# Two blocks and a routed expert layer on one core: one fixed first expert instead of two, the order of the others worked out earlier, twelve weight slots, a new order of passes

## The chip, the core and the metric

One core of a Trainium2 chip runs one program. The metric is its time in microseconds on the device. Engines: TensorE (PE; its weight loads are listed as PEld), VectorE (DVE), ScalarE (ACT), GpSimd (POOL) and the sync engine (SP), which issues the large loads. Transfers run on 16 DMA engines.

## What is computed

`reference` runs two blocks over 512 rows of 1024. The first mixes a gated convolution and a linear recurrence, the second is attention followed by an expert layer. The change is in the expert layer, which is in essence:

```python
logits = h @ w_router + b_router                     # 512 rows, 32 experts
top_val, top_idx = top_k(logits, 4); gates = softmax(top_val)
# the rows of each expert, 2048 places in all
hgu = xs @ w_gate_up[e] + b_gate_up[e]               # 1024 x 2048
act = clamped_swiglu(hgu)
out = (act @ w_down[e] + b_down[e]) * gate           # 1024 x 1024
h = layernorm(alpha * h + sum over the 4 experts of out)
```

Inputs and outputs are float32. Each expert has 12 MB of weights, so the layer reads 32 x 12 MB.

## The kernel before

**Passes.** The expert stage runs 32 passes, one for each expert. Passes 0 and 1 are experts 0 and 1 (STATIC = 2). The other 30 experts are put in order of their number of rows, and each place in that order (rank) is given to a pass of a fixed kind by a table (`moe`, from `_tables`, line 42): the two ranks with most rows go to PAIRS (8, 18), the next ten to large passes, then 15 to SMALL and the last three to TINY. Kinds differ in rows and in arithmetic. A large pass holds 128 rows; each weight tile is split by ScalarE (line 128) and VectorE (line 129) into a high and a low part, and three products are summed (`products`, lines 1894 to 1920). A small pass holds 64 rows and a tiny one 32; they multiply the raw float32 tile and put the column blocks side by side in the array (`small_products`, line 1867). A pair is a large pass with a further tiny tile of 32 rows on the same raw weights. An expert with more rows than its pass holds gets further tiles in a loop at the end (`further_tiles`, line 1979).

**Units and their order.** A pass has a way up (gate and up weights, 8 units of 1 MB) and a way down (4 units of 1 MB). Block b of the loop at line 2048 runs the way up of pass b and then the way down of pass b - 1 (`units`, line 282). So the weights are used in the order: up 0, up 1, down 0, up 2, down 1 and so on. `beside` (line 1924) puts the other steps of neighbouring passes before or in the middle of a unit's products: `place` and `fetch` (which rows), `gather` (an indirect load on the POOL queue), `xpose` and `xparts` (transposing the rows on TensorE and copying them), `glu`, `at_T` and `at_parts` (the gate function and the transposed activations), `finish` (scaling by the gate on ScalarE, then a scatter-add to memory on the POOL queue). Each engine works through its own instructions in the order written.

**Weights.** `Weights` (line 86) holds a list of loads to do and a list of free raw slots of 1 MB. `issue` takes the first load and the first slot and issues the load on the sync queue; it is called when a slot is released. A large pass releases a raw slot when the tile is split, a small or tiny one after the unit's products, a pair after the products of both tiles. `ahead` and `beyond` split up to two units ahead into three pairs of split buffers. There are RAW + RAWK + RAWX = 2 + 7 + 2 = 11 slots; the last two lie in the pool `pM`, whose memory is free once the attention's residual has been stored.

**The order of the experts.** `order` (line 1643) runs in steps beside pass 0: it compares all 32 x 32 keys (count x 32 - index) in one VectorE operation, sums them to ranks, turns ranks and counts into columns by TensorE, builds a permutation matrix and permutes the lists. Its result `pm_i` is read by the sync engine (`expert`, line 1969) for the address of each load of an ordered pass, first for unit 20. Rows of passes 0 and 1 are gathered ahead of the loop (lines 1562, 2036 to 2040), so the rows of pass 1 are there before pass 0 begins.

## Time and profile before

| | us |
|---|---|
| median of 3 runs (1916.35 to 1921.56) | 1917.02 |
| the profiled execution | 1921.13 |
| its span, first to last instruction | 1919.4 |
| busy: TensorE, VectorE, ScalarE, POOL | 1723.4, 1153.2, 774.8, 512.7 |
| read from and written to memory | 488.8 MB and 20.1 MB |

All rows are from the profiled execution, in microseconds from the start of its span. A busy TensorE includes the time that a matmul is drawn out by what it waits for inside, so a busy share near 100% doesn't say that it runs at its peak. "DMA share" is the busy share of the 16 DMA engines; overlapping packets make it exceed 1 slightly. The granted clock of TensorE has a mean of 0.951 of full speed over the span.

### The profile page before, as it was taken

How to read it: one execution, taken by the hardware profiler on the slowest of the kernel's cores; microseconds unless marked ns; L12 is line 12 of the kernel's file. 1: busy time of each engine (PE TensorE's matmuls, PEld its weight loads, DVE VectorE, ACT ScalarE, POOL GpSimd, SP SyncE). 2: the span in 40 equal slices, each digit the busy share in tenths (PEclk: the TensorE clock that was granted, in tenths of full speed). 3: DMA queues.
4: the chain of work that ended last, by engine and by line, in shares of the span. 5: the costliest groups of instructions: out<-in, count | busy, mean ns of one | idle time of the engine just before them, and what ended most of it. 6: DMA issues, size and time to landing. Idle time of an engine off the chain costs nothing. (4 is left out here: it accounts for less than half of the span.)

```text
span 1919.4 us, 23312 instructions
## 1 busy us (share of the span) xinstructions
PE 1723.4 (90%) x8751; PEld 1144.0 (60%) x8751; DVE 1153.2 (60%) x1448; ACT 774.8 (40%) x910; POOL 512.7 (27%) x400
## 2 busy tenths in 40 slices
PE   4899886979898899899998898999989899999995
PEld 3687664758787677776552455456445565767531
DVE  6799984775746556798440444347345466767513
ACT  5223533733335444364420333335233354556301
POOL 3899995540311221401101001011010110101002
PEclk8999898989998899899999898999999999999998
DMA  8322221254221005688999999999998999999994
GB/s 296 88 72 71 77 88 59 95 198 154 89 61 55 1 1 177 263 310 326 410 396 395 389 350 378 404 403 406 402 387 340 384 406 411 405 395 406 376 408 160
DMA packets 127508, 503.52 MB, mean 262 GB/s; under 512 B 15350, under 2 KB 57908, under 8 KB 79776
## 3 DMA queue, kind: packets, MB, share of 16 engines
q1 hardware_dynamic: 115568, 475.22, 63.5%
q0 software_dynamic: 11088, 25.39, 4.8%
q8 instruction: 70, 1.15, 0.2%
q10 hardware_dynamic: 736, 1.38, 0.2%
q14 instruction: 46, 0.38, 0.1%
HBM read 488.80 MB, written 20.10 MB: 265 GB/s over the span
## 5 line engine op out<-in xcount | busy, mean ns | idle before, releaser
L129 DVE TENSOR_TENSOR wlo<-wraw,whi 128x2048 fp32r<-128x2048 f32 (+1 forms) x213 | 486.5, 2292 | 161.6 <-ACT whi L128 151.7
L128 ACT CAST whi<-wraw 128x2048 fp32r<-128x2048 f32 (+1 forms) x213 | 401.7, 1891 | 172.0 <-PE pg L1907 56.4
L1889 PE MATMUL pg<-wraw,xTs 128*64 128x512 f32 (+1 forms) x1600 | 259.1, 514 | 4.9 <-DMA wraw<-w_gate_up 4.8
L1889 PEld LDWEIGHTS pg<-wraw,xTs 128*64 128x64 f32 (+1 forms) x1600 | 82.7, 126 | 150.5 <-issue 117.8
L1618 DVE TENSOR_SCALAR lp<-pg 128x512 f32<-128x512 f32 (+1 forms) x48 | 31.6, 659 | 195.7 <-ACT sg L1617 195.7
L1889 PE MATMUL pg<-wraw,ats 128*64 128x512 f32 (+1 forms) x800 | 141.0, 528 | 8.7 <-issue 5.4
L1907 PE MATMUL pg<-whi,xTh 128*128 128x512 f32 x448 | 127.7, 407 | 13.4 <-ACT whi L128 13.4
L1548 POOL DMA_INDIRECT xg<-h_d,ix x34 | 57.9, 1702 | 284.2 <-issue 109.4
L544 POOL TENSOR_TENSOR acc<-acc,sparel 128x512 f32<-128x512 f32 x91 | 129.1, 1419 | 7.7 <-ACT acc L533 0.2
L1625 POOL DMA_INDIRECT acc_d<-y,back x19 | 30.2, 1591 | 371.6 <-ACT y L1861 312.0
L1907 PE MATMUL pg<-whi,xTl 128*128 128x512 f32 x448 | 125.5, 402 | 0.0
L1907 PE MATMUL pg<-wlo,xTh 128*128 128x512 f32 x448 | 122.4, 395 | 0.0
L1907 PEld LDWEIGHTS pg<-whi,xTh 128*128 128x128 f32 x448 | 83.3, 192 | 41.5 <-ACT whi L128 14.3
L1625 POOL DMA_INDIRECT acc_d<-y,ix x14 | 25.1, 1793 | 298.2 <-ACT y L1864 235.5
L537 DVE SCALAR_TENSOR_TENSOR pc<-v,C,pc 128x512 f32<-128x512 f32 x144 | 101.6, 747 | 2.1 <-ACT pc L533 0.8
L1617 ACT ACTIVATE sg<-pg 128x512 f32<-128x512 f32 (+1 forms) x48 | 26.4, 574 | 189.2 <-PE pg L1889 114.4
L542 POOL TENSOR_SCALAR sparel<-v,C 128x512 f32<-128x512 f32 x91 | 97.9, 1076 | 14.8 <-DVE V L459 6.2
L1907 PEld LDWEIGHTS pg<-wlo,xTh 128*128 128x128 f32 x448 | 85.2, 190 | 19.3
L1907 PEld LDWEIGHTS pg<-whi,xTl 128*128 128x128 f32 x448 | 84.0, 192 | 17.8 <-issue 0.4
L1889 PEld LDWEIGHTS pg<-wraw,ats 128*64 128x64 f32 (+1 forms) x800 | 39.6, 127 | 78.5 <-issue 56.7
L1918 PE MATMUL pg<-whi,ath 128*128 128x512 f32 x224 | 75.6, 419 | 1.6 <-ACT whi L128 1.6
L1918 PE MATMUL pg<-wlo,ath 128*128 128x512 f32 x224 | 71.7, 402 | 3.1 <-DVE wlo L129 3.0
(662 smaller groups left out, 3336.8 us busy)
## 6 DMA issues: line engine op xcount, KB each, us to landing
wraw<-w_gate_up SPq DMA_DIRECT2D x256, 1024.0 KB, 17.7
wraw<-w_down SPq DMA_DIRECT2D x128, 1024.0 KB, 18.7
wraw<-w_in SPq DMA_DIRECT2D x17, 1024.0 KB, 5.3
wraw<-w_out SPq DMA_DIRECT2D x8, 1024.0 KB, 5.0
mraw<-mod_w SPq DMA_DIRECT2D x7, 1024.0 KB, 15.5
wraw<-w_in SPq DMA_DIRECT2D x14, 512.0 KB, 5.3
wraw<-pw_w SPq DMA_DIRECT2D x4, 1024.0 KB, 5.1
wraw<-mod_w SPq DMA_DIRECT2D x4, 1024.0 KB, 5.0
```

The costliest lines, as they stand in the source:

```text
L128: self.nc.scalar.copy(out=hi[:, c], in_=t[:, c])
L129: self.nc.vector.tensor_tensor(out=lo[:, c], in0=t[:, c], in1=hi[:, c].bitcast(F32), op=OP.subtract)
L537: dve.scalar_tensor_tensor(out=acc[:, c, :] if j == 29 and not np_ else st_["o"], in0=v[:, j:j + S], scalar=dw_col(j, c), in1=st_["o"], op ...
L542: pool.tensor_scalar(out=pr_, in0=v[:, j:j + S], scalar1=dw_col(j, c), scalar2=0.0, op0=OP.mult, op1=OP.add)
L544: pool.tensor_tensor(out=acc[:, c, :], in0=acc[:, c, :], in1=pr_, op=OP.add)
L1548: pool.indirect_dma_start(out=xg, out_offset=None, in_=h1_d[:, :], in_offset=bass.IndirectOffsetOnAxis(ap=ix[0:w], axis=0), bounds_check=S ...
L1617: act.activation(out=sg, in_=v2[:, :, :, 0], func=AF.Sigmoid, scale=1.702)
L1618: dve.tensor_scalar(out=lp, in0=v2[:, :, :, 1], scalar1=-6.0, scalar2=8.0, op0=OP.max, op1=OP.min)
L1625: pool.indirect_dma_start(out=dst, out_offset=bass.IndirectOffsetOnAxis(ap=ix, axis=0), in_=y, in_offset=None, bounds_check=nt * S - 1, oo ...
L1889: pe.matmul(o, l, t[:, c0:c0 + n_], start=False, stop=u == 3 and k == 1 if dn else u == 7)
L1907: pe.matmul(it["acc"][c // 2][:, c % 2, :], l, r[:, 512 * c:512 * c + 512], start=False, stop=u == 7 and j == 2)
L1918: pe.matmul(it["acc"][2][:, c, :], l, r[:, c0:c0 + 512], start=False, stop=end)
```

## The change

1. STATIC is 1: only expert 0 has a fixed pass. The other 31 experts are ordered; the new table has pairs at passes 3 and 9, tiny passes at 1, 4 and 10, 16 further small ones, and large ones at 5, 7 and then at every odd pass from 11 to 25. There are ten ordered large passes as before, and one more small one.
2. The ranks are worked out ahead of the gates, by one comparison of a row of keys with a column of keys (the counts also come as a column, from 16 one-column matmuls), and `pm_i` is there before the loop. `order` keeps only the permutation of the lists.
3. The way down of pass 0 is loaded right behind its way up, ahead of the way up of pass 1 (`late` gives a load's place in the order of use); the loads of all later passes are listed before the loop.
4. RAWX is 3, so there are 12 raw slots; row buffers, one product buffer and the row parts have one copy less, and a pair's second tile has an output buffer of its own (`yt`).
5. The rows of pass 1 are gathered in block 0 (gather ahead of unit 5, transposes in the middle of unit 7, copies behind it), no longer ahead of the loop. The gates of pass 0 follow ahead of unit 5.

The diff without its context lines:

```diff
@@ -32,10 +32,10 @@
-STATIC = 2
-PAIRS = (8, 18)
-SMALL = (2, 3, 5, 6, 7, 9, 11, 12, 14, 16, 17, 19, 21, 23, 26, 29, 30, 31)
-TINY = (2, 9, 19)
+STATIC = 1
+PAIRS = (3, 9)
+SMALL = (1, 2, 4, 6, 8, 10, 12, 14, 16, 18, 20, 22, 24, 26, 27, 28, 29, 30, 31)
+TINY = (1, 4, 10)
@@ -73,13 +73,17 @@
-    moe = np.zeros((128, 66), f)
+    moe = np.zeros((128, 67 + NE), f)
+    least = np.arange(NE) + 131072.0 * (np.arange(NE) < STATIC)
+    moe[:, 66] = least[p % NE]
+    moe[:, 67:] = least
@@ -91,26 +95,34 @@
-    def add(self, *loads, split=True, n=2048, pieces=1):
-        self.todo.append((loads, split, n, pieces))
+        self.last, self.used = 0, 0
+    def add(self, *loads, split=True, n=2048, pieces=1, late=0):
+        self.todo.append((loads, split, n, pieces, self.last + late))
+        self.last += 1
+    def ready(self):
+        return self.raw and self.raw[0][-1] == self.used
     def issue(self):
-        loads, split, n, pieces = self.todo.pop(0)
+        loads, split, n, pieces, at = self.todo.pop(0)
-        self.raw.append((t, split, n, pieces, slot))
+        self.raw.append((t, split, n, pieces, slot, at))
+        self.raw.sort(key=lambda r: r[-1])
     def split(self):
-        t, s, n, pieces, slot = self.raw.pop(0)
+        t, s, n, pieces, slot, _ = self.raw.pop(0)
+        self.used += 1
@@ -138,12 +150,12 @@
     def ahead(self, n):
-        while len(self.part) < n and self.raw:
+        while len(self.part) < n and self.ready():
     def beyond(self, n):
-        while self.raw and len(self.part) < n:
+        while self.ready() and len(self.part) < n:
@@ -206,7 +218,7 @@
-    RAW, RAWK, RAWX = 2, 7, 2
+    RAW, RAWK, RAWX = 2, 7, 3
@@ -296,18 +308,23 @@
     def rows2(w, pairs):
-    def add_unit(p, dn, u, of):
+    def add_unit(p, dn, u, of, late=0):
         def src():
-        W.add((kn(2, 1024) if dn else flat, src), split="both" if p in PAIRS else p not in SMALL)
+        W.add((kn(2, 1024) if dn else flat, src), split="both" if p in PAIRS else p not in SMALL,
+              late=late)
-    for p in range(STATIC):
-        add_block(p, lambda e: (w_gu[e], w_dn[e]))
+    FIRST = lambda e: (w_gu[0], w_dn[0])
+    for p, dn, u in units(0):
+        add_unit(p, dn, u, FIRST)
+    for u in range(4):
+        add_unit(0, True, u, FIRST, 8)
...
@@ -1491,6 +1508,10 @@
+    for j in range(4):
+        for i in range(4):
+            pe.matmul(pp_[NE * i:NE * i + NE, 5 * NE:5 * NE + 1], sel[:, j, :], trib[:, 1, 0:1], start=(j == 0),
+                      stop=(j == 3))
@@ -1560,9 +1581,29 @@
+    pmr = pK.tile([128, NE], F32, name="pmr")
+    pm_i = pK.tile([1, NE], I32, name="pm_i")
+    Pk = pK.tile([128, NE], F32, name="Pk")
+    pcol = pK.tile([128, 2], F32, name="pcol")
+    ky = lrep.rearrange("p i e -> p (i e)")
+    key, gtr, kc = ky[:, 0:NE], ky[:, NE:2 * NE], ky[:, 2 * NE:2 * NE + 1]
+    dve.tensor_copy(out=pcol[:, 1:2], in_=pp_[:, 5 * NE:5 * NE + 1])
+    dve.scalar_tensor_tensor(out=key, in0=cnt, scalar=float(NE), in1=moe[:, 67:], op0=OP.mult, op1=OP.subtract)
+    dve.scalar_tensor_tensor(out=kc, in0=pcol[:, 1:2], scalar=float(NE), in1=moe[:, 66:67], op0=OP.mult,
+                             op1=OP.subtract)
+    dve.tensor_scalar(out=gtr, in0=key, scalar1=kc, scalar2=None, op0=OP.is_gt)
+    dve.tensor_reduce(out=pcol[:, 0:1], in_=gtr, axis=mybir.AxisListType.X, op=OP.add)
+    dve.tensor_scalar(out=Pk, in0=moe[:, 0:NE], scalar1=pcol[:, 0:1], scalar2=None, op0=OP.is_equal)
+    pp1 = psa("pperm")
+    pe.matmul(pp1[:, 0:NE], sq5[0:NE, 4, 65:66].to_broadcast([NE, 128]), Pk[0:NE], start=True, stop=True)
+    pe.matmul(pp1[:, NE:2 * NE], pcol[0:NE, 1:2].to_broadcast([NE, 128]), Pk[0:NE], start=True, stop=True)
+    dve.tensor_copy(out=pm_i, in_=pp1[0:1, 0:NE])
+    dve.tensor_copy(out=pmr, in_=pp1[:, 0:NE])
+    dve.tensor_copy(out=cnt, in_=pp1[:, NE:2 * NE])
@@ -1602,8 +1643,7 @@
-    def transposed(xg, a):
-        pt = psa("pxt")
+    def transposed(xg, a, pt):
@@ -1613,7 +1653,7 @@
-        lp = pM.tile([128, 2, 256], F32, tag="lp", name="lp", bufs=2)[:, 0:a, 0:n]
+        lp = pM.tile([128, 2, 256], F32, tag="lp", name="lp")[:, 0:a, 0:n]
@@ -1636,46 +1676,20 @@
     def into(parts, k, src):
-    pmr = pK.tile([128, NE], F32, name="pmr")
-    pm_i = pK.tile([1, NE], I32, name="pm_i")
     def order():
-        io = sq5[:, 4, 1:1 + NE]
-        key, r = [wk[:, NE * j:NE * j + NE] for j in range(2)]
-        pcol = wk[:, 7 * NE + 2:7 * NE + 4]
-        Pk, Pb, pT = wk[:, 256:288], wk[:, 288:416], wk[:, 512:768]
-        rows = wk[:, 768:1024]
-        gt_ = pM.tile([128, NE, NE], BF16, tag="xi", name="gt_")
-        pt = psa("pord")
+        Pb, pT = wk[:, 288:416], wk[:, 512:768]
+        pt = pss("pord")[:, 0, :]
-        dve.scalar_tensor_tensor(out=key, in0=cnt, scalar=float(NE), in1=io, op0=OP.mult, op1=OP.subtract)
-        for e in range(STATIC):
-            dve.memset(key[:, e:e + 1], -float(NE * (e + 1)))
-        yield
-        dve.tensor_tensor(out=gt_, in0=key.unsqueeze(1).to_broadcast([128, NE, NE]),
-                          in1=key.unsqueeze(2).to_broadcast([128, NE, NE]), op=OP.is_gt)
+        yield
-        yield
-        dve.tensor_reduce(out=r, in_=gt_, axis=mybir.AxisListType.X, op=OP.add)
-        for j, row in enumerate((r, cnt)):
-            dve.tensor_copy(out=rows[0:1, 128 * j:128 * j + 128].rearrange("p (i e) -> p i e", i=4),
-                     in_=row[0:1].unsqueeze(1).to_broadcast([1, 4, NE]))
-        yield
-        pc = psa("pcol")
-        for j in range(2):
-            pe.matmul(pc[:, j:j + 1], rows[0:1, 128 * j:128 * j + 128], ones[0:1, 0:1], start=True, stop=True)
-        dve.tensor_copy(out=pcol, in_=pc[:, 0:2])
-        dve.tensor_scalar(out=Pk, in0=moe[:, 0:NE], scalar1=pcol[:, 0:1], scalar2=None, op0=OP.is_equal)
-        pe.matmul(pp2[:, 0:NE], sq5[0:NE, 4, 65:66].to_broadcast([NE, 128]), Pk[0:NE], start=True, stop=True)
-        pe.matmul(pp2[:, NE:2 * NE], pcol[0:NE, 1:2].to_broadcast([NE, 128]), Pk[0:NE], start=True, stop=True)
@@ -1685,9 +1699,6 @@
-        dve.tensor_copy(out=pm_i, in_=pp2[0:1, 0:NE])
-        dve.tensor_copy(out=pmr, in_=pp2[:, 0:NE])
-        dve.tensor_copy(out=cnt, in_=pp2[:, NE:2 * NE])
@@ -1769,7 +1780,7 @@
     def fetch(n):
-        it["pi"] = rows_at(it["oh"], it["cols"], 0, 5 if n > 1 else 2)
+        it["pi"] = rows_at(it["oh"], it["cols"], 0, 5)
@@ -1779,8 +1790,7 @@
-        if n > 1:
-            it["gt"] = gates_of(it["pi"])
+        it["gt"] = gates_of(it["pi"])
@@ -1788,21 +1798,25 @@
     def xpose(n):
-        it["pt"] = transposed_rows(it["xg"]) if small(n) else [transposed(it["xg"], a) for a in range(2)]
-    def x_tile(n=9):
-        return xT_[n] if n < 2 else [pM.tile([128, 8, 128], F32R, tag=t, name=t, bufs=2) for t in ("xTh", "xTl")]
+        if small(n):
+            it["pt"] = transposed_rows(it["xg"])
+        else:
+            pt = pss("pxt") if n == 0 else None
+            it["pt"] = [transposed(it["xg"], a, pt[:, a, :] if n == 0 else psa("pxt")) for a in range(2)]
+    def x_tile():
+        return [pM.tile([128, 8, 128], F32R, tag=t, name=t) for t in ("xTh", "xTl")]
     def xparts(n):
-            xp = pM.tile([128, 8, 128 // small(n)], F32, tag="xTh", name="xTs", bufs=2)
+            xp = pM.tile([128, 8, 128 // small(n)], F32, tag="xTh" if small(n) == 2 else "xTs", name="xTs")
-        xp = x_tile(n)
+        xp = x_tile()
...
@@ -1855,7 +1869,7 @@
     def finish(n):
-        y = pM.tile([128, D], F32, tag="y", name="y")
+        y = pM.tile([128, 256], F32, tag="yt", name="y") if PLACES[n][1] else pM.tile([128, D], F32, tag="y", name="y")
@@ -1944,15 +1958,19 @@
-            before[7] += [(late_gates, 0), (late_gates, 1), (place, 2)]
-            midst[7].append((fetch, 2))
-            midst[4].append((xpose, 1))
-            before[5].append((xparts, 1))
+            before[4].append((place, 1))
+            midst[4].append((fetch, 1))
+            before[5] += [(gather, 1), (late_gates, 0)]
+            before[8].append((place, 2))
+            midst[7].append((xpose, 1))
+            before[8].append((xparts, 1))
-                if j or b == 1 and n != 2:
+                if j:
+                if b == 1:
+                    midst[1].append((fetch, n))
...
@@ -2030,21 +2048,21 @@
-    xT_ = [[pM.tile([128, 8, 128], F32R, tag=t, name=t, bufs=2) for t in ("xTh", "xTl")] for _ in range(2)]
-    place(1)
-    fetch(1)
-    gather(1)
+    for p, dn, u in units(1):
+        if not dn:
+            add_unit(p, dn, u, of, -4)
+    for b in range(2, NE + 1):
+        add_block(b, of)
-    next(ordering)
@@ -2087,9 +2105,6 @@
-                if j == 6:
-                    for n in range(STATIC, NE + 1):
-                        add_block(n, of)
```

## Rows read from the trace of the kernel before

**Rows 1.** The page: memory traffic in 40 slices of 48 us.
```profile
GB/s 296 88 72 71 77 88 59 95 198 154 89 61 55 1 1 177 263 310 326 410 396 395 389 350 378 404 403 406 402 387 340 384 406 411 405 395 406 376 408 160
```

**Rows 2.** Stretches: length, busy time by engine, clock, DMA share, GB/s.
```profile
815.00:850.00 35.00, 30.86 (x153) 23.35 (x151) 30.76 (x39) 19.86 (x16) 0.17 (x1) 0.99 0.85 314
850.00:894.00 44.00, 44.00 (x296) 33.20 (x298) 37.44 (x49) 25.23 (x24) 4.29 (x3) 1.00 0.79 291
894.00:1080.00 186.00, 165.61 (x814) 77.54 (x807) 74.83 (x98) 48.62 (x52) 20.50 (x15) 0.94 1.02 401
1080.00:1130.00 50.00, 48.21 (x382) 27.57 (x383) 22.10 (x27) 16.48 (x20) 5.33 (x3) 1.00 0.90 327
1130.00:1420.00 290.00, 269.67 (x1388) 147.99 (x1381) 138.72 (x149) 107.63 (x101) 32.29 (x20) 0.96 1.01 401
1420.00:1470.00 50.00, 48.21 (x389) 27.41 (x391) 22.10 (x27) 16.50 (x20) 4.94 (x4) 1.00 0.87 316
...
1640.00:1780.00 140.00, 139.78 (x650) 94.16 (x649) 103.92 (x96) 80.99 (x68) 15.39 (x8) 1.00 1.00 399
1780.00:1800.00 20.00, 20.00 (x99) 11.79 (x99) 9.83 (x14) 6.38 (x10) 1.57 (x1) 1.00 0.91 354
...
757.00:1882.00 1125.00, 1060.36 (x5703) 621.39 (x5701) 606.34 (x711) 441.41 (x419) 132.13 (x83) 0.97 0.97 380
```

**Rows 3.** DMA queue of the loads, 1640:1780: packets, MB, share.
```profile
q1 hardware_dynamic: 7366, 53.62, 93.9%
```

**Rows 4.** Stretches: large up, pair up, large down, small up, down.
```profile
1755.20:1778.60 23.40, 22.76 (x96) 17.82 (x96) 1.00 1.02 399
1079.10:1112.60 33.50, 24.34 (x96) 17.40 (x96) 1.00 0.93 343
...
1778.70:1791.30 12.60, 11.81 (x48) 8.79 (x48) 1.00 1.01 419
...
1793.00:1808.70 15.70, 14.39 (x64) 4.33 (x64) 1.00 0.90 315
1839.00:1847.10 8.10, 7.31 (x32) 2.12 (x32) 1.00 1.01 422
```

**Rows 5.** Timeline of the sync queue: start, length, line, count.
```profile
873.96 15.21 SPq L105 DMA_DIRECT2D wraw<-w_down  x4
890.03 9.80 SPq L105 DMA_DIRECT2D wraw<-w_gate_up  x8
```

**Rows 6.** DMA issues, whole run and at 868.4: median us to landing.
```profile
wraw<-w_gate_up SPq DMA_DIRECT2D x256, 1024.0 KB, 17.7
...
wraw<-w_gate_up SPq DMA_DIRECT2D x1, 1024.0 KB, 5.4
```

**Rows 7.** Gather issued at 863.94: us to landing; TensorE's timeline.
```profile
xg<-h_d,ix POOLq DMA_INDIRECT x1, 7.5
...
905.23 1.08 PE L1602 MATMUL pxt<-sq,xg 64*128 64x64 f32 x8 [4.51 <-DMA xg<-h_d,ix]
...
1071.78 1.05 PE L1602 MATMUL pxt<-sq,xg 32*128 32x32 f32 x8 [6.85 <-DVE xTl L201]
```

**Rows 8.** Timeline ahead of the first products: VectorE, TensorE.
```profile
811.09 0.29 DVE L1505 TENSOR_REDUCE gs<-rt 128x4 f32<-128x128 f32 x1
...
819.93 0.66 PE L1608 MATMUL pxt<-sq,xg 128*128 128x128 f32 x4 [1.87 <-DVE xTl L201]
...
821.18 1.20 PE L1907 MATMUL pg<-whi,xTh 128*128 128x512 f32 x4
```

**Rows 9.** POOL's DMA queue, 813:822, 899.9:904.9, 893:898: packets, MB.
```profile
q0 software_dynamic: 288, 0.38, 15.7%
...
q0 software_dynamic: 80, 0.26, 17.9%
...
q0 software_dynamic: 139, 0.13, 14.6%
```

**Rows 10.** Timeline of ScalarE behind the first pair.
```profile
1162.66 0.47 ACT L1861 ACTIVATE y<-pg,gt 128x256 f32<-128x256 f32 x1 [11.14 <-DMA acc_d<-y,ix]
```

More of the change, by code (lines that the diff above doesn't have):

```diff
@@ L1335, in block_kernel @@
     xg2 = [pK.tile([128, D], F32, name=f"xg{i}") for i in range(2)]
-    moe = pK.tile([128, 66], F32, name="moe")
+    moe = pK.tile([128, 67 + NE], F32, name="moe")
     sp.dma_start(out=moe, in_=A["t_moe"])
@@ L1836, in at_parts @@
                 if n == NI - 1:
-                    it["at"] = pM.tile([128, 8, 128], F32, tag="xTh", name="ats", bufs=2)[:, 0:4]
+                    it["at"] = pM.tile([128, 8, 128], F32, tag="xTl", name="ats")[:, 0:4]
                 elif PLACES[n][1]:
@@ L2001, in further_tiles @@
                 se = oer.to_broadcast([128, 128])
-                xT = pM.tile([128, 8, 128], F32R, tag="xTh", name="xTf", bufs=2).bitcast(F32)
+                xT = pM.tile([128, 8, 128], F32R, tag="xTh", name="xTf").bitcast(F32)
                 for a in range(2):
-                    k, src_ = transposed(xg, a)
+                    k, src_ = transposed(xg, a, psa("pxt"))
                     act.copy(out=xT[:, k, :], in_=src_)
```

## The prediction

> **What bounds the kernel now.** I read the slices of the page first: from slice 18 (816 us) to the slice before the last the GB/s line stands at 310 to 411 [rows 1]. So the expert stage, over half of the span, moves weights nearly all the time. The chain of waits that the page gives covers only the last dozen microseconds and says nothing of that stage. I cut the stage into stretches instead [rows 2]. There are two kinds. In the full ones (894:1080, 1130:1420, 1640:1780) the DMA share is 1.00 to 1.02 at 399 to 401 GB/s. In the others it falls: 815:850, 850:894, 1080:1130, 1420:1470, 1780:1800. One weight unit is 1.049 MB; 53.62 MB in the 140 us of the fullest long stretch is 51.1 units, 2.74 us each, gathers and scatters included [rows 3]. There are 384 units. The stage ends when the last has landed (about 1882), and the 37 us from there to the end of the span are untouched by the change.
>
> Second, how near TensorE is. A large pass takes 23.4 us for its way up and 12.6 for its way down, a small one 15.7 and 8.1, a pair 33.5 for its way up [rows 4]. 12 units at 2.74 take 32.9 us. So a small pass (23.8) and a large beside a small (59.8 against 65.8) wait for DMA, two larges and a small (95.8 with the gaps of about 0.5 us: 99) just exceed it (98.7), and a pair's way up (4.19 us a unit) is far slower than DMA. DMA is the bound, and what can be won is DMA time that stands empty because every raw slot holds something. Against 401 GB/s the stretches lose: 815:850 (1 - 314/401) x 35 = 7.6 us; 850:894 12.1; 1080:1130 9.2; 1420:1470 10.6; 1780:1800 2.3. Together 41.8 us. DMA also rests ahead of 815, until the last pool's slots exist; the change keeps that.
>
> **The change part by part.** *Early part of the stage.* Before, passes 0 and 1 are both large and hold a split weight each 2.9 us, so units are issued at about that pace; pass 2, a tiny one, frees its eight slots only from 887 on, and the queue, which issues four units in 15 us from 873.96, issues eight in the 10 us from 890.03 [rows 5]. After, pass 1 is tiny and runs right behind pass 0's way up: 821.18 [rows 8] + 23.4 [rows 4] + 3.4 (next paragraph) + 2 for the row parts, near 850. Units 0 to 7 (way up), 8 to 11 (way down, loaded ahead) and 12 to 19 (pass 1) fill the slots: seven are freed by pass 0's splits, one more is the twelfth. They land by about 847, as the nineteenth does now. Then nothing can be issued until pass 1 frees its first slot, near 851.5; with 5.4 us from issue to landing on an empty queue [rows 6] unit 20 lands near 857. From there I take 2.7 us a unit. So of 850:894 I keep about 5 us and win 7. The twelfth slot is worth one unit in 815:850: 2.6 us.
>
> The price of this order is a shorter way for pass 1's rows. Their gather stands ahead of unit 5 and TensorE's transposes of them in the middle of unit 7, 2.3 units (6.7 us) later. The gather's VectorE steps come behind a split, about 1.4 us into the unit, the POOL instruction 1.1 us on, and 7.5 us to landing [rows 7]: 10 us together. So TensorE waits about 3.4 us there, with two thirds of unit 7 and all of pass 1 queued behind it, and VectorE and ScalarE (the gate functions) behind those. This is in the 850 above. The second such wait, for pass 2's rows in pass 0's way down, replaces the one that is there now, 4.51 us [rows 7].
>
> *The ordering of the experts.* It adds ten small VectorE operations of at most 0.29 us each [rows 8], with a trip over TensorE (two small matmuls) that VectorE waits for, ahead of the gates, and 16 one-column matmuls. It lies under the gather of pass 0's rows. Against it, pass 1's one-hot and index no longer stand ahead of the two splits, and both transposes go into one large PSUM tile, so that the second no longer waits 1.87 us [rows 8]. No row shows the new chain: from 1.87 us sooner to 4 us later (2.9 and an estimated 1 for the trip) for the first product. I take 0, as the gather and the warming matmuls cover most of it; if that cover is gone, the 4 us fall on the early part. The sync queue now reads the order before unit 12, not 20; behind that read stand all later loads. The list should be ready near 814, the last pool's slots come at 815, so it costs nothing; without that cover it delays every load by what it is late.
>
> *One large pass becomes small.* TensorE loses 36.0 - 23.8 = 12 us of work, which alone wins nothing where DMA is the bound. The bytes stay: 32 experts are read in full. The extra-tile loop stays empty: pass 3 gathers 0.26 MB, 64 rows of 4 KB, so rank 12 exactly fills its 64 places; expert 1 has at most 60 rows (both fixed passes gather 0.38 MB, 92 rows, of which pass 0 scatters 32, 0.13 MB [rows 9]) and falls in behind it.
>
> *The pairs.* After, they stand at 3 and 9. A unit takes 17.7 us from issue to landing when the queue is full [rows 6], so about six are in flight and, of 11 slots, five hold landed units when a pair begins; its way up of 33.5 us then takes eight of the 12 units that DMA could bring. The new pass 3 starts near 897 (850, a tiny way up of some 9, 12.6 and 4.5 for pass 0's way down, 15.7, 5) with about four landed and eight of 12 slots in flight, two more than now: 9.2 - 2 x 2.74 = 3.7 stay. At pass 9 only the twelfth slot helps: 10.6 - 2.6 = 8. Won: 8.1 us. The output buffer of its own for a pair's second tile takes away a ScalarE wait of 11.14 us behind each pair [rows 10], which held up the next large pass; the DMA queue stayed full there (1130:1420 at 401), so I count nothing, and behind pass 3 it helps TensorE catch up.
>
> *The order behind them.* Large and small alternate from 11 to 25 and six small ones end it, so two larges never stand together: the 2.3 us of 1780:1800 go. The single buffers for rows and products are rewritten only after their readers in the same engine's order: nothing.
>
> **The sum.** 2.6 + 7 + 8.1 + 2.3 = 20 us. The profiled execution took 1921.1 (span 1919.4); 1901 for it. The median is 4.1 lower, so 1897.
>
> At one place a rule speaks against this. The full stretches read and write 399 to 401 GB/s for up to 290 us [rows 2]. The Trainium skill, "DMA: Bandwidth & Descriptors", Specifications, gives about 358 GB/s as the limit of HBM for one core. By it the 427 MB of 757:1882 (1125 us at 380 GB/s) would take 1193 us, more than the 1125 measured, and there would be no empty time to win; the trace disagrees, and its 401 is used; the second rival below has the same time.
>
> **The rivals.**
> *Half of it is given back* (0.16): pass 3 keeps its 9.2 us and the waits for rows take 5 more of the early part; 20 - 5.5 - 5 = 9.5 us, 1907. For it: waits of 4.51 and 6.85 us in TensorE's order behind other engines [rows 7]. Against: each is under three units.
> *The mean rate can't rise* (0.13): the whole stage holds 380 GB/s [rows 2]; if memory or the queue caps the mean near it, or units come at 2.8 us once DMA never rests, 330 units lose 20 us: 1917, no change. Against: three stretches of 140 us and more at 399 to 401.
> *Slower* (0.07): a large pass whose first split waits for its landing holds ScalarE, so the row parts, so TensorE's transposes: 6.85 us now, ahead of pass 8 [rows 7]. From 11 to 25 the new order has eight larges, each behind a small or tiny one. If at each the slots fill meanwhile, 8 x 6.85 = 55 us more: 1897 + 55 = 1952. It decides when such a wait exceeds what is in flight: seven units of 2.74, less two, 14 us. None in the trace comes near, and the stretch with the 6.85 kept 401 GB/s.
> *Everything empty goes* (0.05): 1917 - 41.8 = 1875.
>
> **How the numbers follow.** My forecast has 0.59; its own range is 1886 to 1907: 0.02 us a unit over some 330 units is 7, the ordering's ends are 2 and 4. The range given, 1881 to 1914, leaves out the slower rival, part of the flat one and the best case. About 0.3% (6 us) is what a measurement here tells from no change. Faster: 0.59 + 0.05 + 0.12 of the halved gain; same: 0.13 + 0.04; slower 0.07.
>
> **What would show it.** After: units landing at 2.7 us without a break from about 857; no stretch under 360 GB/s but one near pass 9; TensorE waiting some 3 us for gathered rows near 845; no ScalarE wait of 11 us behind a pair; the last unit landing near 1862. I am wrong if DMA still stands at 290 GB/s before 895, if a full stretch falls under 390, or if work of the extra-tile loop appears.

## The result, and the profile after

| | before | changed |
|---|---|---|
| median (four runs each, side by side) | 1918.76 us | 1892.58 us |
| ratio, 95% interval | | 0.9858 [0.9841, 0.9875] |
| the same again, other runs (nine and four) | 1919.77 us | 1894.87 us, 0.9857 [0.9839, 0.9876] |
| profiled execution, its span | 1921.13, 1919.4 us | 1887.72, 1885.8 us |

The forecast was 1897, 20 us less than before; it came out at 26.2 us less (24.0 to 30.5 by the interval). Below, a kernel's distance from the changed one is taken from 1893.4 us, the median of its eight runs. Each ratio has an interval of some 0.0015 to either side, 3 us, so a difference between two experiments holds to about 4 us.

The slices of the page, kernel after (memory traffic, 47 us each): the dips of [rows 1] at 350, 387, 340, 384 and 376 are gone. The eighteenth slice reads 265 where it read 310, but it covers 801 to 849 now and covered 816 to 864 before; the stretches below have the same bounds in both, and the stage begins 5.3 us sooner now.

```profile
GB/s 301 90 73 73 78 90 45 112 135 213 59 104 56 1 1 110 298 265 365 390 395 412 399 413 398 403 403 411 420 402 406 404 404 396 403 406 396 406 414 132
```

Stretches of the kernel after, columns as in [rows 2] (length, busy time by engine, granted clock, DMA share, GB/s):

```profile
815.00:850.00 35.00, 29.69 (x158) 21.69 (x160) 18.76 (x28) 14.06 (x14) 2.81 (x1) 0.95 0.66 259
850.00:894.00 44.00, 39.39 (x300) 19.85 (x292) 27.00 (x47) 13.27 (x15) 4.73 (x4) 1.00 0.97 376
894.00:1080.00 186.00, 182.06 (x1190) 109.08 (x1192) 110.61 (x127) 79.13 (x78) 26.47 (x16) 0.99 1.00 398
930.00:950.00 20.00, 18.35 (x151) 8.01 (x153) 7.04 (x13) 3.50 (x8) 1.63 (x1) 1.00 0.89 345
1080.00:1130.00 50.00, 48.49 (x314) 32.07 (x311) 31.64 (x23) 25.99 (x19) 4.16 (x2) 1.00 1.01 413
1130.00:1420.00 290.00, 282.22 (x1531) 165.98 (x1530) 166.75 (x171) 129.68 (x121) 34.44 (x19) 0.99 1.02 407
1420.00:1470.00 50.00, 50.00 (x239) 31.44 (x239) 30.88 (x32) 22.13 (x22) 6.25 (x3) 1.00 1.01 400
...
1780.00:1800.00 20.00, 16.47 (x72) 4.50 (x68) 0.00 (x0) 0.75 (x2) 2.57 (x2) 1.00 1.02 399
```

Against 401 GB/s, as in the prediction, what stands empty is 12.4 us in 815:850, 2.7 in 850:894, 2.8 in 930:950 (behind the pair at pass 3) and 0.1 in 1780:1800: 18.0 us where it was 41.8. So 23.8 of the 33.6 us between the two profiled spans are empty DMA time that is gone. Another 5.3 come from ahead of the stage: the first weight load is issued at 751.75 instead of 757.02, which the change doesn't cause (last section). From that issue to the last landing the stage takes 1097.5 us instead of 1125.4, 28.0 less, so some 4 are left beside the 23.8; 1130:1420, at 407 GB/s instead of 401, is worth 4.3, and the other stretches gain or lose some 1.5 us each.

What waits for what has turned over. The sums of waits of the kernel before, and of the one after (engine, line, waited for: us in total, times, longest):

```profile
ACT whi L128 <- DMA wraw<-w_down: 26.5, 10, 9.3
ACT whi L128 <- DMA wraw<-w_gate_up: 20.4, 4, 7.9
ACT y L1861 <- DMA acc_d<-y,ix: 21.7, 2, 11.1
```
```profile
ACT whi L140 <- DMA wraw<-w_down: 73.8, 27, 8.7
PEld pg L1903 <- DMA wraw<-w_gate_up: 33.1, 31, 3.0
POOL acc_d L1665 <- DMA acc_d<-y,ix: 17.5, 2, 9.1
```

The splits and the small products now stand waiting for the experts' weights to land more than before: 73.8 against 26.5 and 20.4 us for the splits. ScalarE's wait for the scatter behind the pairs is gone; it is now POOL, about to issue the next scatter, that waits for it. More of the stage is limited by DMA than before.

### The profile page after: what moved, and what is told of

The parts are those of the page before. It is cut to its first block, busy times and chain, and to the rows that moved or that the text cites. A ratio compares the mean times of both kernels' runs of the same rounds, so it can differ in the third digit from the quotient of the medians.

```text
span 1885.8 us, 23223 instructions
## 1 busy us (share of the span) xinstructions
PE 1701.9 (90%) x8713; PEld 1111.8 (59%) x8713; DVE 1118.5 (59%) x1425; ACT 751.9 (40%) x894; POOL 516.0 (27%) x400
## 5 line engine op out<-in xcount | busy, mean ns | idle before, releaser
L141 DVE TENSOR_TENSOR wlo<-wraw,whi 128x2048 fp32r<-128x2048 f32 (+1 forms) x201 | 457.0, 2282 | 152.9 <-ACT whi L140 146.7
L140 ACT CAST whi<-wraw 128x2048 fp32r<-128x2048 f32 (+1 forms) x201 | 379.6, 1891 | 193.6 <-DMA wraw<-w_down 73.8
L1903 PE MATMUL pg<-wraw,xTs 128*64 128x512 f32 (+1 forms) x1664 | 274.6, 516 | 12.0 <-DMA wraw<-w_gate_up 12.0
L1903 PE MATMUL pg<-wraw,ats 128*64 128x512 f32 (+1 forms) x832 | 145.0, 524 | 6.3 <-DMA wraw<-w_down 3.8
L1921 PE MATMUL pg<-whi,xTh 128*128 128x512 f32 x416 | 116.2, 401 | 0.4 <-issue 0.4
L1921 PE MATMUL pg<-whi,xTl 128*128 128x512 f32 x416 | 114.8, 398 | 0.0
L1921 PE MATMUL pg<-wlo,xTh 128*128 128x512 f32 x416 | 113.2, 394 | 0.0
L1657 ACT ACTIVATE sg<-pg 128x512 f32<-128x512 f32 (+1 forms) x47 | 25.7, 573 | 184.3 <-PE pg L1903 101.1
L1921 PEld LDWEIGHTS pg<-whi,xTh 128*128 128x128 f32 x416 | 75.9, 188 | 26.0 <-issue 10.6
L1921 PEld LDWEIGHTS pg<-wlo,xTh 128*128 128x128 f32 x416 | 78.7, 189 | 17.7
L1921 PEld LDWEIGHTS pg<-whi,xTl 128*128 128x128 f32 x416 | 76.6, 188 | 16.3
L213 DVE TENSOR_TENSOR atl<-pat,ath 128x256 fp32r<-128x256 f32 x52 | 20.0, 421 | 92.4 <-ACT ath L212 92.4
## 6 DMA issues: line engine op xcount, KB each, us to landing
wraw<-w_gate_up SPq DMA_DIRECT2D x256, 1024.0 KB, 20.4
```

Of the source, the lines that this page charges most:

```text
L140: self.nc.scalar.copy(out=hi[:, c], in_=t[:, c])
L141: self.nc.vector.tensor_tensor(out=lo[:, c], in0=t[:, c], in1=hi[:, c].bitcast(F32), op=OP.subtract)
L1657: act.activation(out=sg, in_=v2[:, :, :, 0], func=AF.Sigmoid, scale=1.702)
L1903: pe.matmul(o, l, t[:, c0:c0 + n_], start=False, stop=u == 3 and k == 1 if dn else u == 7)
L1921: pe.matmul(it["acc"][c // 2][:, c % 2, :], l, r[:, 512 * c:512 * c + 512], start=False, stop=u == 7 and j == 2)
```

## The experiments

All but two are the changed kernel with an edit; the two that begin with b are the kernel before with a part of the change.

| | median, us | ratio to before | to the changed kernel |
|---|---|---|---|
| e1: 11 slots | 1900.38 | 0.9913 [0.9900, 0.9925] | +6.9 |
| e2: old order of passes | 1897.75 | 0.9897 [0.9882, 0.9911] | +4.3 |
| e3: one output buffer | 1903.37 | 0.9930 [0.9916, 0.9944] | +9.9 |
| e4: loads in order of use | 1892.77 | 0.9875 [0.9859, 0.9891] | -0.7 |
| e5: old order, one buffer | 1899.19 | 0.9900 [0.9882, 0.9918] | +5.7 |
| e6: pass 1 large | 1911.57 | 0.9947 [0.9934, 0.9961] | +18.1 |
| e7: old order, one buffer, 11 slots | 1905.18 | 0.9925 [0.9911, 0.9939] | +11.7 |
| b1: before, new order alone | 1917.92 | 0.9992 [0.9982, 1.0002] | |
| b2: before, own buffer alone | 1917.56 | 0.9993 [0.9983, 1.0003] | |
| v1: pairs at 9 and 17 | 1893.38 | 0.9871 [0.9852, 0.9891] | -0.1 |
| v3: rows of pass 1 sooner | 1889.71 | 0.9831 [0.9815, 0.9846] | -3.7 |

The medians come from three sets of runs, in which the kernel before had 1918.1, 1919.0 and 1919.8. By the ratios, each to the kernel before in its own set, e1, e2 and e3 stand some 10.6, 7.6 and 13.9 us above the changed kernel, not 6.9, 4.3 and 9.9: the signs hold, the sizes are good to 4 us.

A second table is a further witness: the time between the issues of certain loads (the first is 0, the last 383), worked out from the sync queue's issue of each of the 384 in the traces. It leaves out what happens ahead of the stage. Each row is one execution, and the two of the changed kernel differ by 3.4 us in all.

| us from load to load | 0 to 20 | 20 to 44 | 44 to 96 | 96 to 212 | 212 to 383 |
|---|---|---|---|---|---|
| before | 91.2 | 73.7 | 135.1 | 330.5 | 474.1 |
| changed | 98.7 | 56.8 | 140.0 | 316.9 | 464.7 |
| changed, second profile | 99.1 | 58.1 | 139.7 | 318.8 | 464.8 |
| e1: 11 slots | 101.1 | 59.3 | 139.3 | 320.4 | 465.6 |
| e2: old order | 99.3 | 50.8 | 143.9 | 322.1 | 470.5 |
| e3: one buffer | 97.7 | 57.6 | 145.0 | 322.1 | 464.8 |
| e4: loads in order of use | 99.2 | 56.5 | 139.7 | 319.9 | 464.8 |
| e5: old order, one buffer | 98.1 | 50.7 | 144.5 | 320.9 | 472.6 |
| e6: pass 1 large | 90.9 | 87.5 | 139.1 | 320.4 | 464.9 |
| e7: as e5, 11 slots | 102.3 | 51.6 | 143.1 | 324.9 | 471.3 |
| b1: before, new order | 91.1 | 81.9 | 140.4 | 321.7 | 470.7 |
| b2: before, own buffer | 91.5 | 73.3 | 135.0 | 327.6 | 473.2 |
| v1: pairs at 9, 17 | 98.8 | 50.1 | 142.8 | 325.6 | 459.8 |
| v3: rows sooner | 96.1 | 56.4 | 140.5 | 316.9 | 464.8 |

**The twelfth slot**

```diff
-    RAW, RAWK, RAWX = 2, 7, 3
+    RAW, RAWK, RAWX = 2, 7, 2
```

> The changed kernel with 11 raw slots instead of 12, nothing else. If the gain is DMA time that no longer stands empty for want of a free slot, one slot less costs one unit (2.74 us) wherever the queue runs dry: ahead of pass 1, where every slot is full from 843 to 850, behind pass 3, where the loads in flight fall to 1 at 942, and perhaps behind pass 9, where they fall to 2 at 1140. So 5 to 8 us over the changed kernel, about 1899, and the stretch behind pass 9 falls under 400 GB/s. If the slot is worth nothing (the new order alone keeps the queue full), 0 to 2 us. If the twelfth slot is what carries the pairs, both pairs dip as before and 15 us or more are lost.

6.9 us slower. The second table puts 3 to 5 of them into the first 44 loads and 2 to 4 into 96 to 212, where pass 9 stands; 1130:1200, at 394 GB/s in the changed kernel, falls to 366:

```profile
1130.00:1200.00 70.00, 68.22 (x518) 42.86 (x518) 40.90 (x41) 31.40 (x31) 9.49 (x6) 1.00 0.96 366
```

So a slot is worth about a unit at each place where the queue runs dry, as worked out, and not the 15 us of the other theory.

**The order of the passes**

```diff
-PAIRS = (3, 9)
+PAIRS = (8, 18)
-SMALL = (1, 2, 4, 6, 8, 10, 12, 14, 16, 18, 20, 22, 24, 26, 27, 28, 29, 30, 31)
-TINY = (1, 4, 10)
+SMALL = (1, 2, 3, 5, 6, 7, 9, 11, 12, 14, 16, 17, 19, 21, 23, 26, 29, 30, 31)
+TINY = (1, 9, 19)
```

> The changed kernel with the table of passes of the kernel before as far as one fixed pass allows: pairs at 8 and 18, two larges together at 24/25 and 27/28, pass 1 tiny. If the new order of the passes is what keeps the queue full, both pairs run dry again: by the working of the prediction 6.5 us at pass 8 and 7.9 at pass 18 with the twelfth slot, 2.3 at the two larges, less the 3 that pass 3 now loses, so 13 to 14 us over the changed kernel, 1906, with stretches of 320 to 350 GB/s around the pairs. If the gain at the pairs comes from the slot and from the separate output buffer of the tiny tile instead, the order is worth 0 to 4 us.

4.3 us slower by the medians, where 13 to 14 were expected. The dips at the pairs do come back, at the places of the kernel before (327 and 316 GB/s there, [rows 2]):

```profile
1080.00:1130.00 50.00, 47.78 (x409) 26.73 (x402) 25.59 (x31) 17.85 (x20) 5.18 (x3) 1.00 0.94 361
1420.00:1470.00 50.00, 47.77 (x410) 26.95 (x412) 26.02 (x30) 17.39 (x21) 4.98 (x3) 1.00 0.93 349
```

That is 5.0 and 6.5 us empty, against 2.8 behind pass 3 and 1.1 behind pass 9 in the changed kernel: 7.6 us more. The second table has between 6 and 10. All are short of 13. The two larges side by side, for which 2.3 were counted, lose nothing any more: 1640:1800 moves 398 GB/s and more.

**The output buffer of a pair's tiny tile**

```diff
-y = pM.tile([128, 256], F32, tag="yt", name="y") if PLACES[n][1] else pM.tile([128, D], F32, tag="y", name="y")
+y = pM.tile([128, D], F32, tag="y", name="y")
```

> The changed kernel with the output of a pair's tiny tile back in the buffer of the others, so that ScalarE waits again for the scatter ahead of it, 11 us behind each pair. By the prediction that wait lies under a full queue and costs nothing (0 to 1 us; a wait of some 11 us on ScalarE shows behind passes 3 and 9). If it is what the prediction missed at pass 9 (no dip at all where 8 us were expected to stay), the stretch behind pass 9 falls under 380 GB/s and 5 to 9 us are lost; behind pass 3, where the queue is already near empty, up to 4.

9.9 us slower: the prediction's "nothing" was wrong here. ScalarE's timeline behind both pairs of e3 has the waits again:

```profile
991.29 0.47 ACT L1875 ACTIVATE y<-pg,gt 128x256 f32<-128x256 f32 x1 [10.53 <-DMA acc_d<-y,ix]
...
1197.41 0.47 ACT L1875 ACTIVATE y<-pg,gt 128x256 f32<-128x256 f32 x1 [11.33 <-DMA acc_d<-y,ix]
```

During the first of them DMA loses nothing (960:1000 and 1000:1080 move 403 and 406 GB/s). What it costs is the reserve: TensorE, held up by 10 us, leaves landed units in their slots, and the next loads go out later. Counted from the first load of each, load 72 of e3 is issued 9.4 us later than in the changed kernel. Load 114, for which a split of pass 7 frees the slot, is only 1.5 later, but load 116, the first for which pass 9 frees one, is 6.7 later. TensorE reaches this next pair late by as much. Its first products, in the changed kernel and then in e3:

```profile
1099.80 1.20 PE L1921 MATMUL pg<-whi,xTh 128*128 128x512 f32 x4
```
```profile
1113.29 1.19 PE L1921 MATMUL pg<-whi,xTh 128*128 128x512 f32 x4
```

Counted from the first load (751.75 and 758.51) that is 348.1 and 354.8 us. While TensorE is late nothing more is issued and the loads on their way go on landing, so the pair begins with five in flight instead of eight. There the time is lost. The stretch behind pass 9, first in e3, then in the changed kernel:

```profile
1130.00:1160.00 30.00, 27.91 (x204) 14.42 (x192) 11.52 (x18) 5.54 (x9) 4.14 (x2) 1.00 0.83 307
```
```profile
1130.00:1160.00 30.00, 28.21 (x270) 13.71 (x269) 16.39 (x24) 12.15 (x16) 2.61 (x2) 1.00 1.00 386
```

7.0 us against 1.1 empty (2.8 in the second profile of the changed kernel). The second wait makes load 144 17.7 us late, and from load 210 on 8 to 13 us stay (5 to 9 against the second profile). In the changed kernel pass 9 begins at 1100 with eight loads in flight and ends with two at 1140; in the kernel before, the pair at 1079 begins with six and is down to one from 1104 to 1116 (counted from issues and landings; where a load has no record of landing, it is put between its neighbours).

**Loads in the order of use**

```diff
-    for u in range(4):
-        add_unit(0, True, u, FIRST, 8)
...
-    W.prefetch()
...
-    for p, dn, u in units(1):
-        if not dn:
-            add_unit(p, dn, u, of, -4)
-    for b in range(2, NE + 1):
+    for b in range(1, NE + 1):
         add_block(b, of)
+    W.prefetch()
```

> The changed kernel with the loads in the order in which the units are used: pass 1's way up ahead of pass 0's way down, so that units from the ninth on wait for the order of the experts (about 812). Two loads that now start at 769 and 779 start at 812 instead. From 815 on DMA has time for them, since every slot is full and nothing is issued from 838 to 850.5: twelve units at 2.74 from 817 are there by 850. So 0 to 3 us by the theory of full slots. If bytes moved early are worth their time whenever they are moved, two units, 5.5 us.

No difference (-0.7 us): loading the first way down ahead wins nothing that can be measured. Load 20, the first that waits for pass 1, goes out 99.2 us after the first load, against 98.7 and 99.1 in the changed kernel: DMA has time for the others before that anyhow.

**Order and buffer, alone and undone together**

b1 is the new order in the kernel before, b2 the buffer in it:

```diff
-PAIRS = (8, 18)
-SMALL = (2, 3, 5, 6, 7, 9, 11, 12, 14, 16, 17, 19, 21, 23, 26, 29, 30, 31)
-TINY = (2, 9, 19)
+PAIRS = (3, 9)
+SMALL = (2, 4, 6, 8, 10, 12, 14, 16, 18, 20, 22, 24, 26, 27, 28, 29, 30, 31)
+TINY = (2, 4, 10)
```

> The kernel before with the new order of passes alone (pairs at 3 and 9, tiny passes at 2, 4 and 10, small and large in turn from 11 to 25); two fixed large passes, 11 slots and one output buffer stay. The prediction gave the order at the pairs and the two larges together some 8 us without the slot's part: 1910. By what the runs so far show, the order lives on the slot (7.8 us without it) and on the tile's own output buffer (10.8 us without it): changed time 1892.6 and both of these and some 5 to 7 us of the early part make 1916 to 1918, that is 0 to 2 us gained; ScalarE then waits some 11 us behind both pairs and the loads in flight stay at 2 or 3 for 20 us after that.

```diff
-        lp = pM.tile([128, 2, 256], F32, tag="lp", name="lp", bufs=2)[:, 0:a, 0:n]
+        lp = pM.tile([128, 2, 256], F32, tag="lp", name="lp")[:, 0:a, 0:n]
-        y = pM.tile([128, D], F32, tag="y", name="y")
+        y = pM.tile([128, 256], F32, tag="yt", name="y") if PLACES[n][1] else pM.tile([128, D], F32, tag="y", name="y")
```

> The kernel before with the tiny tile's own output buffer alone (one product buffer less makes the room for it). The wait of 11 us on ScalarE behind each pair goes. If that wait costs by itself whatever the order, 8 to 10 us are gained, 1909. If it costs only where the next pair comes before the queue is full again, as it does from pass 3 to 9 in the new order, the old order with ten passes between its pairs gains 0 to 4 us: 1914 to 1918.

e5 joins the edits of e2 and e3.

> The changed kernel with the old order of passes and without the tiny tile's own output buffer: both undone at once. If the buffer is worth its 10.8 us in either order, 1897.8 and 10.8: 1908. If it is worth them only in the new order, 1898 to 1902, and then the new order is no gain at all without the buffer (1903.4 with the new order and one buffer).

In the kernel before neither part changes the time alone: 1.1 and 1.4 us under 1918.99, and both intervals hold 1. Behind b1's unchanged total, though, the second table has 13.4 us lost up to load 96, where a pair now stands behind two large passes, and 12.2 won after it. In the changed kernel the four combinations are:

| us | own buffer | one buffer |
|---|---|---|
| new order | 1893.4 | 1903.4 |
| old order | 1897.8 | 1899.2 |

The sums of the second table are 1077.1 and 1080.5 (new order, own buffer), 1087.2 (new order, one buffer), 1086.6 and 1086.8 (old order). In both, the buffer is worth 7 to 10 us in the new order and 0.2 to 1.4 in the old one, and with it the new order is 4 to 10 us faster than the old one. That the new order is slower without it isn't shown: 4 us by the medians, 0.4 by the sums.

The old order has nine passes between its pairs, the new one five. That the nine are enough to catch up can be read from e5 against e2: behind the first pair of e5 load 130 goes out 8.9 us later than in e2, from load 163 on the loads are level or ahead, and load 224 is the first that the second pair frees a slot for.

**Pairs further on**

```diff
-PAIRS = (3, 9)
-TINY = (1, 4, 10)
+PAIRS = (9, 17)
+TINY = (1, 10, 18)
```

> The changed kernel with its pairs at 9 and 17, each with a tiny pass behind it; pass 3 is a large one. In the changed kernel pass 3 begins with 7 loads in flight and runs the queue down to 1; pass 9 begins with 8 and loses hardly anything. If a full queue at the start is what spares a pair, pass 17 (behind a large and a small one, as 9 is) loses as little as pass 9, the 4 to 7 us that pass 3 loses are won, and the time is 1886 to 1889. If a pair costs its 4 to 7 us wherever it stands, the time stays at 1892.

No difference (-0.1). Loads 0 to 96 go 4 to 5 us faster without a pair at 3, but pass 17, which begins at 1365 with eight loads in flight too, still costs 5.1 us behind it:

```profile
1370.00:1420.00 50.00, 48.22 (x414) 27.12 (x406) 22.89 (x29) 16.86 (x20) 5.21 (x3) 1.00 0.98 360
```

Pass 9 of v1 begins with some seven loads in flight, and it too loses 5.1 us (333 GB/s in 1120:1150, 391 in the changed kernel). So a full queue at its start isn't enough to spare a pair. Why pass 9 of the changed kernel loses so little stays open in part: the buffer and the slot are necessary for it (e3, e1), but they aren't all, since v1 has both.

**A large pass 1**

```diff
-SMALL = (1, 2, 4, 6, 8, 10, 12, 14, 16, 18, 20, 22, 24, 26, 27, 28, 29, 30, 31)
-TINY = (1, 4, 10)
+SMALL = (2, 4, 6, 8, 10, 12, 14, 16, 18, 20, 22, 24, 25, 26, 27, 28, 29, 30, 31)
+TINY = (2, 4, 10)
```

> The changed kernel with a large pass 1 instead of a tiny one; passes 2, 4 and 10 are tiny and 25 is small, so the numbers of each kind stay. Pass 1 then releases its slots at the pace of its splits, 2.9 us each, and pass 0's way down behind it at 3.1, so the queue can't refill until pass 2. If the tiny pass 1 is what won the early part, 7 us are lost, 1899, and 850 to 894 falls from 376 to some 310 GB/s. If the early part was won by the slot and by having one fixed pass less, 0 to 2 us.

18.1 us slower, far more than 7. Loads 20 to 44 take 87.5 us instead of 57, and the pair at 3, which begins at 933 with four loads in flight (seven in the changed kernel, at 902), is down to one at 950 and 960. The trace is that of the slowest of e6's six runs, 1921.78 us, so the stretches show somewhat more than the median does:

```profile
850.00:894.00 44.00, 37.31 (x162) 28.60 (x160) 33.81 (x33) 25.92 (x22) 2.54 (x1) 0.92 0.70 273
894.00:960.00 66.00, 61.76 (x460) 41.51 (x460) 51.48 (x68) 28.75 (x26) 10.43 (x7) 0.95 0.89 326
```

b1, which also has two large passes ahead of a pair at 3, shows the same (81.9 us for loads 20 to 44). Up to load 96 the early pair costs 13.4 us behind two large passes (b1 against before) and 4 to 5 behind a tiny pass 1 (the changed kernel against v1).

**Only the one fixed pass, the ordering and the loads ahead**

e7 joins the edits of e1, e2 and e3.

> The changed kernel with the old order, one output buffer and 11 slots: of the change only the one fixed pass, the earlier ordering and the first way down loaded ahead are left. By the prediction the slot was worth 2.6 us early and one unit at each pair, 8 in all, whatever the order: 1899.2 and 8 make 1907, and the remaining 12 against the kernel before are the early part. If the slot is worth its 7.8 us only in the new order, 1899 to 1902.

1905.18 us, near the 1907 of the first theory. The slot is worth 6.0 us in the old order too (e7 to e5). What remains of the change in e7 is worth 14.6 us against the kernel before in the same runs, 1919.77.

**The rows of pass 1 one unit sooner**

```diff
-            before[4].append((place, 1))
-            midst[4].append((fetch, 1))
-            before[5] += [(gather, 1), (late_gates, 0)]
+            before[3].append((place, 1))
+            midst[3].append((fetch, 1))
+            before[4] += [(gather, 1), (late_gates, 0)]
```

> The changed kernel with the steps for pass 1's rows (place, fetch, gather, with the gates of pass 0) one unit sooner, the transposes where they are. The rows then land some 3 us sooner and the 2.5 us that TensorE waits for them at 843 go; pass 1 starts by so much sooner and with it the first new load at 850.5. If the first release of pass 1 sets the time of everything behind it, 2 to 2.5 us faster than the changed kernel: 1890. If the queue makes it up later anyway, no difference.

TensorE's wait for these rows, in the changed kernel and then in v3:

```profile
843.35 0.68 PE L1643 MATMUL pxt<-sq,xg 32*128 32x32 f32 x8 [2.52 <-DMA xg<-h_d,ix]
```
```profile
846.42 0.68 PE L1643 MATMUL pxt<-sq,xg 32*128 32x32 f32 x8 [0.18 <-DMA xg<-h_d,ix]
```

In v3's trace the load at 20 goes out 2.6 us sooner after the first one (96.1 against 98.7), and all that come later stay between 1.2 and 3.7 us ahead: nothing gives it back. Its median, 1889.71 us, is the best of this study, 0.9831 [0.9815, 0.9846] of the time before; that it beats the changed kernel by 3.7 us is at the edge of what the runs can tell, the 2.6 in the trace is plain.

**The changed kernel again**

> The changed kernel once more, unedited, for its time beside the other runs of this call: 1892.6, give or take 1.5. In its first profile the first weight load starts at 751.8; in those of the variants that differ from it only behind that point it starts anywhere from 751.3 to 758.5. If that start is chance, this one lies in that range too and its time follows it; if the change moves it, it lies at 752.

1894.87 us. Its first load starts at 756.56 where the first profile had 751.75; the last section shows why.

## Why the prediction was right, and where it wasn't

**The bound.** Right. The gain is DMA time that stood empty, and a shift of 2.6 us in the first load that waits for a slot arrives at the end undiminished (v3). The rival that the mean rate can't rise has fallen: 1130:1420 moves 407 GB/s, and 757:1848 holds 390 where it held 380. The Trainium skill, "DMA: Bandwidth & Descriptors", Specifications, gives about 358 GB/s for one core; the trace disagrees here too. The rival of slower larges has fallen as well: with the larges of the new order in them, the long stretches from 1130 to 1800 hold 399 to 407, and the lowest part, 1130:1160 behind the pair, 386.

**The early part.** The times were near: pass 1's products began at 848.5 (850 foretold), TensorE waited 2.52 us for its rows (3.4), load 20 landed at 855.24 (857). The sum drawn from them was wrong. Load 19 landed at 842.88, so for 12.4 us no weight landed, and from 838 to 850.5 none was issued; the prediction described that hole ("nothing can be issued until pass 1 frees its first slot"), but charged only 5 us of 850:894 for it and left 815:850 as it was, less a unit. In fact 815:850 lost 12.4 us and 850:894 2.7, together 15.1 (15.8 in the second profile) where 10 were allowed: 4.6 won instead of 9.6. By one of its own signs, no stretch under 360 GB/s but one near pass 9, the early part failed too: 815:850 moves 259. The 5 us are as many as the rival that half is given back takes here, but not for its reason, since the wait for the rows was shorter than foretold; its other half, pass 3 keeping 9.2 us, did not come true.

**The ordering.** Zero was taken, with 4 us as the far end; it was near that end. From the stage's first load to the first product went 64.2 us before (757.02 to 821.18 [rows 8]) and 67.2 after (751.75 to 818.90), 3 us more; the three kernels with the old ordering take 64.1 to 64.5, the other eleven 65.8 to 68.0. Of this, 1.9 are there when the warming products begin (56.1 and 58.0 us after the first load). The second transposes' wait of 1.87 us is gone, as foretold, but another, for ScalarE's copy of the lists that `order` transposes, stands in its place:

```profile
818.02 0.50 PE L1372 MATMUL pg<-bias_p,selr 64*128 64x512 f32 x2 [1.99 <-ACT wk L1687]
818.90 1.17 PE L1921 MATMUL pg<-whi,xTh 128*128 128x512 f32 x4 [0.38 <-issue]
```

The cover that was named, the gather and the warming products, didn't hide it.

**The slot.** 2.6 early and a unit at each pair, 8 in all; measured 6.9 (e1; 5 to 9 by the second table) and 6.0 (e7 to e5). Right.

**The pairs and the order behind them.** Take the slot's units out of the 8.1 and 2.3, and the order itself was to win 5.0 us; with the buffer it won 4.3 (e2; 6 to 10 by the second table). Pass 3 lost 2.8 us (3.7 foretold), the two larges lost nothing. Pass 9 was to keep 8 us empty and kept 1 to 3: of the terms that a stretch shows the one furthest off, and in the favourable direction.

**The buffer.** The failed step is "the DMA queue stayed full there, so I count nothing". The first half is true, in e3 as well as before. But a wait under a full queue uses up the reserve, and whether that costs anything is settled at the next heavy pass: in e3 it begins 6.7 us late, with five loads in flight instead of eight. In the old order, from which the argument was drawn, it costs 1.4 us at most (b2, e5); in the new one 9.9 (e3). Without the buffer the change won 14.7 us (e3, 1903.4 against 1918.1 in the same runs), 5 less than foretold; with it 26.2.

**The sum.** Step by step in medians: before 1919.0, e7 1905.2, with the slot (e5) 1899.2, with the buffer (e2) 1897.8, with the order 1893.4: 13.8, 6.0, 1.4 and 4.4, or 11.4, 6.4, 0.2 and 6 to 9.5 by the second table. So the one fixed pass, the ordering and the loads ahead, foretold as the early 7, bring 13.8. That isn't all early: by the second table e7 is 3.0 us ahead of the kernel before at load 96 (297.0 against 300.0), gains 5.6 from 96 to 212 and 2.8 behind that. Some 2 us of this is what two profiles of one kernel differ by. What of it belongs to the large pass that became small, and what to the row and product buffers, no run separates; it stays open. That the total came within some 6 us is in part luck: the early part brought 5 us less than foretold, pass 9 some 5 to 7 more. The end was as foretold: from the last landing, at 1849.22, to the end of the span 36.6 us (37), and no load of the extra-tile loop.

## What to carry to other kernels

Where transfers are the bound, count how many are in flight when a heavy step begins: a wait that costs no bandwidth while it lasts can still cost all of it at the next heavy step, if that comes before the reserve is back. Parts of a change that act through the same reserve don't add up (the buffer alone: 1.4 us in the old order, 10 in the new), so undo them singly and together. A total that doesn't move can hide a loss and a gain, as in b1, so compare by stages too. And a hole that the plan itself describes must be charged to the stretch in which it lies.

## What was not expected of the hardware

Two profiles of the same kernel differ by 4.8 us ahead of the expert stage. The sync queue of the first profile and of the second:

```profile
751.75 4.90 SPq L115 DMA_DIRECT2D wraw<-w_gate_up  x6
```
```profile
756.56 5.30 SPq L115 DMA_DIRECT2D wraw<-w_gate_up  x6
```

The gap grows, and once shrinks, in steps of about 1 to 1.5 us, at places where TensorE's granted clock is lower in one run than in the other: 510:520 (mean 1.00 in the first, 0.83 in the second), 540:560 (1.00 and 0.91), 625:640 (0.89 and 0.77), 640:655 (0.89 and 1.00, which gives 1.5 us back), 655:670 (1.00 and 0.89), 700:712 (1.00 and 0.87). The second of these places more closely, in the first profile and in the second:

```profile
546.00:547.00 1.00, 1.00 (x10) 1.00 (x9) 0.66 (x2) 0.31 (x1) 0.00 (x0) 1.00 0.00 0
547.00:549.00 2.00, 2.00 (x19) 2.00 (x18) 1.30 (x3) 0.64 (x1) 0.00 (x0) 1.00 0.00 0
```
```profile
546.00:547.00 1.00, 1.00 (x7) 1.00 (x6) 0.90 (x1) 0.00 (x0) 0.47 (x1) 0.52 0.16 45
547.00:549.00 2.00, 2.00 (x11) 2.00 (x11) 1.25 (x3) 0.63 (x1) 0.00 (x0) 0.50 0.00 0
```

The same products run at the upper level (2.4 GHz, 1.00) in one and at the lower (1.2 GHz, 0.50 to 0.52) in the other, 19 of them in two microseconds against 11. In both, the engine had just come through twelve small broadcasts with waits of 0.81 and 0.18 us ahead of and behind them. The Trainium skill, "TensorE: Matmul & The Clock Gate", Part 1, says of the start of a kernel that the count of slow matmuls differs from run to run, and puts the cost of that start under 1% of a typical span. Here such a difference shows in the middle of a kernel; it is of that size, 4.8 of 1890 us. It means that the distance of two profiled executions is no measure of a change of this size: 33.6 us between the profiles here, 26.2 between the medians. It is also why the second table counts from the first load.

Second, a scatter-add of a large tile's rows holds its source for long: in e3 its 13 scatters land 10.4 us after their issue (median), ScalarE waited 10.5 and 11.3 us to write the buffer again, and [rows 10] has the same 11.14. An output buffer that is shared by two tiles of one pass costs that wait each time; what the wait costs in time was 1.4 us in one order of the passes and 10 in another.
